# Seven block products instead of eight in the up projection of an fp32 transformer step

## The chip, the cores and the metric

The kernel runs on one core of a Trainium2 chip, in one launch. The metric is device time in microseconds (us). The core has a TensorE (PE in the profile: matmuls, and PEld, the load of their weights), a VectorE (DVE), a ScalarE (ACT), a GpSimd (POOL) and a SyncE (SP) that issues nearly all DMAs. Each takes its instructions in the order in which they stand; they meet at semaphores.

## The reference

One layer of a decoder with d = 1024, for 2048 prompt tokens and 8 x 8 sample tokens that share all weights: windowed attention and a pooling mixer side by side, attention to 256 memory tokens, then the MLP that the change is about, and a final RMSNorm.

```python
h = _rmsnorm(x, g_ffn)
x = x + jnp.square(jax.nn.relu(h @ w_up)) @ w_down      # w_up 1024 x 4096, w_down 4096 x 1024
y = _rmsnorm(x, g_final)
```

All of it is fp32.

## The kernel before

**Tokens.** Three superblocks `s` = 0, 1, 2 of two token blocks each: 384 + 384, 256 + 256 (with the 64 sample tokens beside the second block in attention), 384 + 384. In each superblock follow the input projection ("in"), attention mixed with it, the output projection ("wo"), cross attention (matrices A and B), the up projection ("up", function `up`) and the down projection ("dn", function `down`). Activations lie transposed: 128 channels on the partitions, tokens along the free dimension. `x` (tiles `x0`, `x1`) holds the residual of the two blocks.

**Three matmuls for one.** Every fp32 operand is split into a rounded part and a rest (`hi`, `lo`, type fp32r). `mm3` and `dense` issue hi x hi, hi x lo and lo x hi into one PSUM tile, so a product of a 128-row weight chunk with a block of tokens costs three matmuls; lo x lo is left out.

**The MLP.** The hidden layer of 4096 is cut into 32 chunks of 128, in eight groups `g` of four. `up(g)` makes four chunks, each over k = 8 input chunks (24 matmuls for each token block); `up_evac` takes the PSUM tile: DVE relu and the factor `r3` of the norm, ACT square and rounding (`hi`), DVE the rest (`lo`). `down(g)` adds the product of the four hidden chunks with the weights to `x`, 8 output chunks of 12 matmuls each, one DVE addition from PSUM for each. The gain of the norm is multiplied into the input (`gain`), the norm itself (`r3`) only after the matmul. In superblock 1 both blocks go as one of 512 tokens; in superblock 2 the sample tokens join (through the DRAM buffer `x_s`), and the two blocks are 512 and 320 wide.

**Weights.** `Stream` loads them in a written order: a DMA of 512 KB into a slot `f`, on ACT the rounding into a slot `w`, on DVE the rest into another (`emit`; L134 and L135 of the profile). There are 12 slots `w`, 6 slots `f`, and at most 5 weights stand ready ahead of use.

**Order.** The code is written in a rough order, with work put off to later points (`later`, `flush`); a scheduler then sets the order of the instructions on each engine, within what the slots and the data allow. The first norm of the next superblock (`norm1`) is started while `down(6)` and `down(7)` still run.

Of the kernel before, what the change touches and what calls it, by code (L numbers as in the profile page):

```python
# [14 lines left out]
P = 128  # L15
# [36 lines left out]
def kernel(ctx: ExitStack, tc: tile.TileContext, io, nW=12, nF=6, nT=8):  # L52
# [11 lines left out]
    TS = Slots([sb(f"t{i}", 448) for i in range(nT)])  # L64
    XT = [sb("x0", 3136), sb("x1", 3584)]
# [5 lines left out]
    x_s = drp.tile([P, 8, 64], F32, name="x_s", tag="x_s")  # L71
# [44 lines left out]

    class Stream:
# [6 lines left out]
        def add(self, key, *raw, eng=None):  # L124
            self.items.append((key, raw, eng or nc.vector))

        def emit(self):
            key, raw, eng = self.items.popleft()
            th, tl = WS.get(), WS.get()
            r = FS.get()  # L130
            w = 1024 // len(raw)
            for i, src in enumerate(raw):
                nc.sync.dma_start(r[:, w * i:w * i + w], src)
            nc.scalar.copy(th[:], r[:, 0:1024])  # L134
            eng.tensor_tensor(tl[:], r[:, 0:1024], f32(th[:]), ALU.subtract)  # L135
# [29 lines left out]
    for s in range(3):  # L165
# [103 lines left out]
    class Act:  # L269

        def __init__(self, n, nk=8, more=()):
            self.n, self.nk = n, nk
            w, per = (NB, 4) if n <= NB else (512, 3)
            left = 2 * nk - 2 * len(more)
            self.h = [ACTS.get() for _ in range(-(-left // per))]
            self.t = [t[:, w * i:w * i + w] for t in self.h for i in range(per)][:left]
            self.t += [t[:, 512 * i:512 * i + 512] for t in more for i in range(2)]
# [4 lines left out]
        def lo(self, k, c0=0, c1=None):  # L282
            return self.t[self.nk + k][:, c0:self.n if c1 is None else c1]
# [20 lines left out]
    def dense(keys, blks, hi, lo, evac, head=2, tail=3, after=None, piece=8, seq=None, early=False):  # L304
# [3 lines left out]
        for c, b in seq or order(nch, head, tail, len(blks)):  # L308
# [193 lines left out]
    def norm1(bl, wait=2):  # L502
        n = bl.n
# [18 lines left out]
        later.append([wait, rest])  # L522

    def load_x(bl):
        nc.sync.dma_start(bl.xv[:, :, 0:bl.n], io["x"][:, bl.xo:bl.xo + 8 * bl.n].rearrange("p (k n) -> p k n", n=bl.n))
        if bl.nf > bl.n:
            nc.sync.dma_start(bl.xv[:, :, bl.n:bl.nf], x_s[:])

    def superblock(s, blks, nxt):
# [486 lines left out]
        def sample_cross():  # L1016
# [117 lines left out]
            nc.sync.dma_start(x_s[:], bl.xv[:, :, bl.np:bl.n])  # L1134
# [7 lines left out]
        def add_evac2(c, b, ps):  # L1142
            bl = blks[b]
            nc.vector.tensor_tensor(bl.x(c, 0, bl.np), ps[:, 0:bl.np], bl.x(c, 0, bl.np), ALU.add)
            for p in bl.parts:
                gain(p.x(c), p.fb.h3.hi(c, p.o, p.o + p.n), p.fb.h3.lo(c, p.o, p.o + p.n), vec[:, V_GFFN + c:V_GFFN + c + 1])
            bl.norm.sq(c)

        def after_co(b):
            bl = blks[b]  # L1150
            for hf in range(2):
                ACTS.put(*bl.pt[hf])
            bl.norm.fin()
# [20 lines left out]
        if last:
            assert len(VS.free) == 4
            fbs[0].more = [(vt, WS.get()), (WS.get(),), (WS.get(),)]
        for fb in fbs:
            fb.h3 = Act(fb.n, 8, fb.more[0])

# [5 lines left out]
        run(dense([("B", s, c) for c in range(8)], pbs,  # L1185
# [3 lines left out]
        hid = {}  # L1189

        def up_evac(g):
            def f(c, b, ps):
                fb = fbs[b]
                if (g, b) not in hid:
                    hid[(g, b)] = Act(fb.n, 4, fb.more[1 + g % 2])
                H = hid[(g, b)]
                for p in fb.parts:
                    o, n = p.o, p.n
                    r, q = TS.get(), TS.get()
                    nc.vector.scalar_tensor_tensor(r[:, 0:n], ps[:, o:o + n], 0.0, p.bl.r3[:, p.c0:p.c0 + n], ALU.max, ALU.mult)  # L1200
                    nc.scalar.activation(q[:, 0:n], r[:, 0:n], AF.Square)  # L1201
                    hi, lo = H.hi(c, o, o + n), H.lo(c, o, o + n)
                    nc.scalar.copy(hi, q[:, 0:n])  # L1203
                    nc.vector.tensor_tensor(lo, q[:, 0:n], f32(hi), ALU.subtract)  # L1204
                    TS.put(r, q)
            return f
# [212 lines left out]
```

## Time and profile before

| | |
|---|---|
| runs | 2574.15, 2576.71, 2580.68 us; median 2576.71 us |
| profiled execution | 2575.38 us, of which the span from the first to the last instruction is 2573.6 us |
| granted TensorE clock | 0.996 |
| busy, share of the span | PE 98%, PEld 90%, DVE 54%, ACT 39%, POOL 7% |
| instructions | PE 14241 matmuls, DVE 2797, ACT 2013 |
| DMA | 245.09 MB, 95 GB/s on average |

A busy time is the time in which at least one instruction of the engine was under way. Matmuls overlap, so the mean duration of one (some 340 ns for 384 tokens) is its latency; the time that one costs in a stream is the length of a stretch of like matmuls over their number. In the profile's groups the shape is (partitions x elements), and "idle before" is the idle time of that engine just before the group.

### The profile page before, as it was taken

To read this page: it belongs to the slowest core of one execution; us is meant where nothing else is said; L and a number is where in the kernel's file an instruction comes from. 1 tells how busy PE (TensorE), PEld (TensorE's weight loads), DVE (VectorE), ACT (ScalarE), POOL (GpSimd) and SP (SyncE) were. 2 spreads that over 40 slices of the span, in tenths; PEclk is the share of its full clock that TensorE was granted. 3 is DMA by queue.
4 is the path that set the end of the run, shared out by engine and by line. 5 is a ranking of instruction groups with operands and counts; after the bars stand their busy time and mean duration, and the time that the engine had idled before them with its cause. 6 is when DMAs were issued, how large, how long until landed. Compare 5 with 4: busy or idle time off the path is not lost.

```text
span 2573.6 us, 36150 instructions
## 1 busy us (share of the span) xinstructions
PE 2534.6 (98%) x14241; PEld 2315.0 (90%) x14241; DVE 1388.7 (54%) x2797; ACT 998.9 (39%) x2013; POOL 167.4 (7%) x282
## 2 busy tenths in 40 slices
PE   9999999999999999999999999999999999999997
PEld 8798989999999999896788888899989888888886
DVE  8568545444434468774554546887445444434435
ACT  6666343322222234753442324475344322222222
POOL 0015010000000000411000000024010000000000
PEclk9999999999999999999999999999999999999999
DMA  8833212111111125146722222414111111111101
GB/s 284 266 121 102 91 37 78 66 66 66 58 65 66 50 66 160 50 168 213 283 98 93 97 99 75 155 32 148 42 62 54 66 58 58 63 60 58 58 25 54
DMA packets 97614, 245.09 MB, mean 95 GB/s; under 512 B 18916, under 2 KB 37796, under 8 KB 96420
## 3 DMA queue, kind: packets, MB, share of 16 engines
q1 hardware_dynamic: 97444, 242.78, 28.3%
q8 instruction: 112, 1.84, 0.3%
q14 instruction: 58, 0.48, 0.1%
HBM read 219.79 MB, written 22.95 MB: 94 GB/s over the span
## 4 chain that ended last, share of the span: by engine, by line
PE 56%; DVE 2%; ACT 1%; DMA 1%; POOL 0%; issue 0%; DVEq 0%; POOLq 0%; ACTq 0%
PE mm L318 10%; PE mm L317 10%; PE mm L319 10%; PE mm L114 7%; PE mm L113 7%; PE mm L115 7%; PE aux L724 1%; PE aux L755 1%; DVE x L1253 0%; PE aux L968 0%; PE aux L1052 0%; PE aux L114 0%; DVE w L135 0%; PE aux L113 0%; PE aux L115 0%; PE aux L1090 0%
## 5 line engine op out<-in xcount | busy, mean ns | idle before, releaser
L317 PE MATMUL mm<-act,w 128*128 128x384 f32 (+3 forms) x2528 | 857.1, 339 | 2.5 <-ACT act L679 1.6
L319 PE MATMUL mm<-act,w 128*128 128x384 f32 (+3 forms) x2528 | 851.4, 337 | 1.9 <-DVE w L135 1.9
L318 PE MATMUL mm<-act,w 128*128 128x384 f32 (+3 forms) x2400 | 801.8, 334 | 0.7 <-DVE act L680 0.7
L134 ACT CAST w<-f 128x1024 fp32r<-128x1024 f32 x330 | 346.5, 1051 | 818.2 <-PE mm L114 278.3
L113 PE MATMUL mm<-act,w 128*128 128x384 f32 (+3 forms) x1472 | 506.1, 344 | 3.2 <-ACT t L204 2.2
L115 PE MATMUL mm<-act,w 128*128 128x384 f32 (+3 forms) x1472 | 504.8, 343 | 1.9 <-DVE w L135 1.9
L317 PEld LDWEIGHTS mm<-act,w 128*128 128x128 f32 x2528 | 476.7, 189 | 28.3 <-ACT act L679 1.9
L319 PEld LDWEIGHTS mm<-act,w 128*128 128x128 f32 x2528 | 476.4, 188 | 23.1 <-DVE w L135 2.7
L135 DVE TENSOR_TENSOR w<-f,w 128x1024 fp32r<-128x1024 f32 x330 | 402.7, 1225 | 154.7 <-ACT w L134 76.9
L318 PEld LDWEIGHTS mm<-act,w 128*128 128x128 f32 x2400 | 452.6, 189 | 21.1 <-issue 2.5
L114 PE MATMUL mm<-act,w 128*128 128x384 f32 (+3 forms) x1344 | 454.1, 338 | 0.0
L1235 DVE TENSOR_TENSOR x<-mm,x 128x384 f32<-128x384 f32 (+2 forms) x448 | 199.2, 468 | 297.3 <-PE mm L115 297.2
L113 PEld LDWEIGHTS mm<-act,w 128*128 128x128 f32 x1472 | 277.1, 188 | 25.3 <-ACT t L204 2.4
L115 PEld LDWEIGHTS mm<-act,w 128*128 128x128 f32 x1472 | 277.1, 188 | 23.0 <-DVE w L135 2.3
L114 PEld LDWEIGHTS mm<-act,w 128*128 128x128 f32 x1344 | 253.0, 188 | 15.8
L1200 DVE SCALAR_TENSOR_TENSOR t<-mm,t 128x384 f32<-128x384 f32 (+3 forms) x224 | 99.8, 468 | 275.6 <-PE mm L319 275.5
L1201 ACT ACTIVATE t<-t 128x384 f32<-128x384 f32 (+3 forms) x224 | 95.1, 450 | 249.8 <-DVE t L1200 249.8
L1204 DVE TENSOR_TENSOR act<-t,act 128x384 fp32r<-128x384 f32 (+3 forms) x192 | 87.8, 477 | 88.9 <-ACT act L1203 88.9
L113 PE MATMUL mm<-w,act 128*128 128x512 f32 x288 | 114.8, 402 | 1.4 <-ACT w L134 1.3
L114 PE MATMUL mm<-w,act 128*128 128x512 f32 x288 | 113.1, 393 | 1.9 <-DVE w L135 1.8
L115 PE MATMUL mm<-w,act 128*128 128x512 f32 x288 | 112.8, 392 | 0.0
L266 ACT ACTIVATE act<-x,vec 128x384 fp32r<-128x384 f32 (+3 forms) x104 | 57.7, 563 | 106.5 <-DVE x L940 56.4
(210 smaller groups left out, 2200.5 us busy)
## 6 DMA issues: line engine op xcount, KB each, us to landing
f<-in_wup SPq DMA_DIRECT2D x96, 512.0 KB, 3.3
f<-in_wdn SPq DMA_DIRECT2D x96, 512.0 KB, 3.2
f<-in_win SPq DMA_DIRECT2D x30, 512.0 KB, 3.5
f<-a_s SPq DMA_DIRECT2D x24, 512.0 KB, 4.2
f<-b_s SPq DMA_DIRECT2D x24, 512.0 KB, 4.2
x<-in_x SPq DMA_DIRECT2D x6, 1536.0 KB, 8.1
f<-in_wco SPq DMA_DIRECT2D x16, 512.0 KB, 5.3
f<-in_cmk SPq DMA_DIRECT2D x16, 512.0 KB, 4.2
```

The costliest lines, as they stand in the source:

```text
L113: nc.tensor.matmul(ps, Wh(k), Hh(k), start=first and i == 0, stop=False)
L114: nc.tensor.matmul(ps, Wh(k), Hl(k), start=False, stop=False)
L115: nc.tensor.matmul(ps, Wl(k), Hh(k), start=False, stop=final and i == last)
L134: nc.scalar.copy(th[:], r[:, 0:1024])
L135: eng.tensor_tensor(tl[:], r[:, 0:1024], f32(th[:]), ALU.subtract)
L317: nc.tensor.matmul(ps[:, 0:n], w8(th)[:, k, :], hi(b, k), start=k == 0, stop=False)
L318: nc.tensor.matmul(ps[:, 0:n], w8(th)[:, k, :], lo(b, k), start=False, stop=False)
L319: nc.tensor.matmul(ps[:, 0:n], w8(tl)[:, k, :], hi(b, k), start=False, stop=k == 7)
L1200: nc.vector.scalar_tensor_tensor(r[:, 0:n], ps[:, o:o + n], 0.0, p.bl.r3[:, p.c0:p.c0 + n], ALU.max, ALU.mult)
L1201: nc.scalar.activation(q[:, 0:n], r[:, 0:n], AF.Square)
L1204: nc.vector.tensor_tensor(lo, q[:, 0:n], f32(hi), ALU.subtract)
L1235: nc.vector.tensor_tensor(p.x(m), ps[:, p.o:p.o + p.n], p.x(m), ALU.add)
```

## The change

The 1024 x 4096 up weight is seen as 16 pairs `p` of hidden chunks. For a pair, the weight is a 2 x 2 matrix of blocks (two halves of the 1024 input channels, two hidden chunks), the input a 2 x 2 matrix of blocks (two halves of the channels, two equal halves of the superblock's tokens). Their product takes seven block products and block sums (Winograd's form of Strassen's algorithm) where it took eight.

- **Token halves** are 384 in superblocks 0 and 2 and 288 in superblock 1 (256 + 32 and 288), where the sample tokens now stay: `x_s` is gone, and superblock 2 has no extra tokens.
- **Sums of inputs**: `B11`, `B21`, `T1`, `T2`, `B22`, `T3`, `T4`, each as hi and lo, made on DVE and ACT once in a superblock, during and just after the product with B (`sums0`, `sums1`, `sums2`); B's chunks come in the order 0, 4, 1, 5, 2, 6, 3, 7 so that the two halves of the channels meet. They lie in 14 of the 16 slots `act`.
- **Sums of weights**: `add_up` loads the pair's two chunks `g.c`, `g.d` and makes three stream items: the split of `g.c`; a DVE sum, a DVE difference and the split of `g.e`; a half split, two more DVE sums and the split of `g.d`. That is three full splits and a half instead of two, and four DVE sums of 512 columns.
- **Sums of outputs**: `up(p)` makes the products into `aux` tiles (which `up` did not use before), each over k = 4 (12 matmuls), and combines them by seven DVE additions and one ACT copy; then relu, square, hi and lo as before (`relu2`).
- **Down projection**: in superblocks 0 and 2 for each pair by itself, k = 2 chunks (6 matmuls for a PSUM tile, one DVE addition for each tile); in superblock 1 for two pairs together (k = 4, 12 matmuls); the last two pairs of each superblock together, one token half after the other.
- **Next superblock's norm**: its first block is started between the last two `up`, its second (`hook`) in the middle of the last `down`. Before, both were started before `down(7)`.
- Slots `t` are 10 of 400 columns instead of 8 of 448.

```diff
+            def first():
+                g.c, g.d = FS.get(), FS.get()
+                nc.sync.dma_start(g.c[:, 0:1024], io["wup"][2 * p])
+                nc.sync.dma_start(g.d[:, 0:1024], io["wup"][2 * p + 1])
+                return split(g.c)
+            def second():
+                g.e = FS.get()
+                nc.vector.tensor_tensor(g.e[:, 0:512], g.d[:, 0:512], g.d[:, 512:1024], ALU.add)
+                nc.vector.tensor_tensor(g.e[:, 512:1024], g.c[:, 0:512], g.e[:, 0:512], ALU.subtract)
+                return split(g.e)
...
+        def sums1(i):
+            e, d = TS.get(), TS.get()
...
+            gain(d[:, 0:hn], T("T1", 0)(i), T("T1", 1)(i), gk(i))
...
-        def up(g):
-            run(dense([("up", s, g, c) for c in range(4)], fbs,
-                      lambda b, k: fbs[b].h3.hi(k), lambda b, k: fbs[b].h3.lo(k), up_evac(g),
+        def up(p, H=None):
...
+            wa = S.next(("up", s, p, 0))
+            p1 = prod(wa, (0, 0), "B11")
+            r1 = TS.get()
+            nc.scalar.copy(r1[:, 0:hn], p1[:, 0:hn])
...
+            wb = S.next(("up", s, p, 1))
+            p5 = prod(wb, (0, 0), "T1")
+            p6 = prod(wb, (512, 512), "T2")
+            r2 = add(TS.get(), p6, r1)
+            r4 = add(TS.get(), p5, r2, False)
+            w22, *wd = S.next(("up", s, p, 2))
+            add(r4, prod(wd, (512, 512), "B22"), r4)
+            relu2(H, 1, 0, r4)
+            p7 = prod(wd, (0, 0), "T3")
+            add(r2, p7, r2)
+            relu2(H, 1, 1, add(TS.get(), p5, r2))
+            p2 = prod(wa, (512, 512), "B21")
+            relu2(H, 0, 0, add(r1, p2, r1))
+            p4 = prod((w22, w22), (0, 512), "T4")
+            relu2(H, 0, 1, add(r2, p4, r2))
...
-                    mm3(ps[:, 0:n], range(4), lambda k: w8(th)[:, 4 * m2 + k, :], lambda k: w8(tl)[:, 4 * m2 + k, :], H.hi, H.lo)
+                    mm3(ps[:, 0:hn], K, lambda k: w8(w[k // 2][0])[:, 2 * m4 + k % 2, :], lambda k: w8(w[k // 2][1])[:, 2 * m4 + k % 2, :],
...
+            for p in range(NP - 2):
+                up(p, H)
+                down([p], [H])
+        up(NP - 2, H)
+        if nxt is not None:
+            S.resF = 4
+            rest0 = norm1_sums(nxt[0])
+        H2 = up(NP - 1)
...
+            later.append([1, rest0])
+            hook = lambda i: norm1(nxt[1], 1) if i == 5 else None
+        down([NP - 2, NP - 1], [H, H2], True, hook)
```

Three places show what the scheduler makes of it. In the rows, L119 is the DVE half of a weight split (L135 before), L190 and L192 are sums of weights, L1292 a sum of outputs from PSUM, L1276 the relu and L1280 the lo part of `relu2` (L1200 and L1204 before), L1350 the addition to `x` in `down` (L1235 before).

On DVE, where an `up` of superblock 0 passes into a `down`, before:

```order
L1200 SCALAR_TENSOR_TENSOR t_101<-mm_107,t_104 128x384
L135 TENSOR_TENSOR w_82<-f_95,w_83 128x1024
L1204 TENSOR_TENSOR act_70<-t_98,act_69 128x384
L1200 SCALAR_TENSOR_TENSOR t_99<-mm_108,t_97 128x384
L1204 TENSOR_TENSOR act_68<-t_100,act_67 128x384
L1200 SCALAR_TENSOR_TENSOR t_102<-mm_109,t_104 128x384
L135 TENSOR_TENSOR w_84<-f_96,w_85 128x1024
L1204 TENSOR_TENSOR act_70<-t_103,act_69 128x384
L1235 TENSOR_TENSOR x_105<-mm_110,x_105 128x384
L1235 TENSOR_TENSOR x_105<-mm_107,x_105 128x384
```

and now, at the last products of a pair (`aux_115` is B21, `aux_116` is T4):

```order
L1292 TENSOR_TENSOR t_98<-aux_115,t_98 128x384
L1276 SCALAR_TENSOR_TENSOR t_104<-t_104,t_106 128x384
L1276 SCALAR_TENSOR_TENSOR t_98<-t_98,t_105 128x384
L1292 TENSOR_TENSOR t_100<-aux_116,t_100 128x384
L192 TENSOR_TENSOR f_91<-f_96,f_92 128x512
L1276 SCALAR_TENSOR_TENSOR t_100<-t_100,t_105 128x384
L1280 TENSOR_TENSOR act_74<-t_104,act_74 128x384
L1280 TENSOR_TENSOR act_73<-t_98,act_73 128x384
L1350 TENSOR_TENSOR x_108<-mm_112,x_108 128x384
L1350 TENSOR_TENSOR x_108<-mm_109,x_108 128x384
L1280 TENSOR_TENSOR act_73<-t_100,act_73 128x384
L119 TENSOR_TENSOR w_86<-f_91,w_79 128x1024
```

Three lo parts that `down` needs now stand behind the sum that waits for T4, the last product, and one of them behind the first two additions of `down`.

On DVE, where superblock 1 ends and the input projection of superblock 2 begins, before:

```order
L540 TENSOR_TENSOR w_84<-kcar,w_85 64x128
L1235 TENSOR_TENSOR x_105<-mm_107,x_105 128x256
L1235 TENSOR_TENSOR x_106<-mm_107,x_106 128x256
L135 TENSOR_TENSOR w_86<-f_93,w_88 128x1024
L208 TENSOR_TENSOR t_98<-t_98,t_97 128x256
L208 TENSOR_TENSOR t_100<-t_100,t_101 128x256
L99 TENSOR_TENSOR w_90<-mm_109,w_89 64x384
```

and now (L263 to L265 are the end of a norm, L300 and L302 the normalised input of the next superblock's second block, L250 the sums of squares and L1371 the output of the final norm; 15 rows like the last five stand between the two pieces):

```order
L1350 TENSOR_TENSOR x_108<-mm_109,x_108 128x288
L263 SCALAR_TENSOR_TENSOR t_100<-t_97 128x384
L263 SCALAR_TENSOR_TENSOR t_103<-t_101 128x256
L264 SCALAR_TENSOR_TENSOR t_100<-aux_113,t_100 128x384
L264 SCALAR_TENSOR_TENSOR t_103<-aux_114,t_103 128x256
L265 SCALAR_TENSOR_TENSOR t_97<-t_100,t_97 128x384
L265 SCALAR_TENSOR_TENSOR t_101<-t_103,t_101 128x256
L300 SCALAR_TENSOR_TENSOR t_105<-f_96,vec,t_97 128x384
L300 SCALAR_TENSOR_TENSOR t_98<-f_96,vec,t_97 128x384
L1371 SCALAR_TENSOR_TENSOR x_107<-x_107,vec,t_101 128x256
L302 TENSOR_TENSOR act_69<-t_105,act_77 128x384
```

```order
L302 TENSOR_TENSOR act_70<-t_102,act_78 128x384
L1371 SCALAR_TENSOR_TENSOR x_107<-x_107,vec,t_101 128x256
L300 SCALAR_TENSOR_TENSOR t_105<-f_94,vec,t_97 128x384
L300 SCALAR_TENSOR_TENSOR t_98<-f_94,vec,t_97 128x384
L119 TENSOR_TENSOR w_85<-f_93,w_87 128x1024
L302 TENSOR_TENSOR act_70<-t_105,act_78 128x384
```

Before, the normalised input was made long before this place; now it is made here, behind the last addition of `down`, and the second weight of the input projection (`w_85`) stands behind it.

On PE, in the input projection of superblock 2 after the change, 44 matmuls after the last one of `down`:

```order
L353 MATMUL mm_109<-act_70,w_80 128x384
L354 MATMUL mm_109<-act_78,w_88 128x384
L352 MATMUL mm_109<-act_78,w_80 128x384
L354 MATMUL mm_112<-act_64,w_85 128x384
L352 MATMUL mm_112<-act_64,w_87 128x384
L353 MATMUL mm_112<-act_67,w_87 128x384
```

PE turns to the second block (`mm_109`, input `act_69`, `act_70`) after the first 24 matmuls, and the fourth of these rows, its 48th matmul after `down`, reads `w_85`; before, all four first weights and both inputs were there, and it went from chunk to chunk.

More of the change, by code (lines that the diff above doesn't have):

```diff
@@ L115, in mm3, with split @@
             nc.tensor.matmul(ps, Wl(k), Hh(k), start=False, stop=final and i == last)
+    def split(r):
+        th, tl = WS.get(), WS.get()
+        nc.scalar.copy(th[:], r[:, 0:1024])
+        nc.vector.tensor_tensor(tl[:], r[:, 0:1024], f32(th[:]), ALU.subtract)
+        return th, tl
+    class FB:
+        pass
     class Stream:
@@ L269, with __init__ @@
     class Act:
[L271 to L277, printed above, removed]
+        def __init__(self, n):
+            self.n = n
+            self.h = [ACTS.get() for _ in range(4)]
+            self.t = [t[:, NB * i:NB * i + NB] for t in self.h for i in range(4)]
         def hi(self, k, c0=0, c1=None):
@@ new lines, in superblock, with tslots, T, f @@
+        hn = halves[1][0][3]
+        PT = 288 if has else NB
+        NAMES = ("B11", "B21", "T1", "T2", "B22", "T3", "T4")
+        tt = {}
+        def tslots(i2, names):
+            for nm in names:
+                tt[(nm, i2)] = ACTS.get()
+        def T(nm, hl):
+            def f(i, c0=0, c1=hn):
+                o = PT * (2 * (i % 2) + hl)
+                return tt[(nm, i // 2)][:, o + c0:o + c1]
+            return f
+        def xp(h, k):
+            return [(bl.x(k, c0, c0 + w), slice(o, o + w), o, o + w) for bl, c0, o, w in halves[h]]
@@ L1174, in superblock @@
[L1174 to L1178, printed above, removed]
+            blks[b].norm.fin()
+            blks[b].r3 = blks[b].norm.r
+        for bl in blks:
+            bl.norm = Norm(bl.n, bl.x)
+        tslots(0, NAMES)
         pbs = []
@@ L1184, in superblock @@
             pbs.append(q)
-        run(dense([("B", s, c) for c in range(8)], pbs,
+        run(dense([("B", s, c) for c in BO], pbs,
                   lambda b, k: k4(blks[b].pt[k // 4][0], blks[b].np)[:, k % 4, :],
                   lambda b, k: k4(blks[b].pt[k // 4][1], blks[b].np)[:, k % 4, :], add_evac2, tail=2, after=after_co))
[L1189 to L1206, printed above, removed]
@@ L1249, in final, with own, relu2 @@
-        def final(p):
-            p.norm.fin()
-            n, yo = p.n, 8 * (p.bl.t0 + p.c0)
+        def own(ts):
+            return [t[:, PT * i:PT * i + hn] for t in ts for i in range(4)]
+        def relu2(H, h, k, t):
+            for bl, c0, o, w in halves[h]:
+                nc.vector.scalar_tensor_tensor(t[:, o:o + w], t[:, o:o + w], 0.0, bl.r3[:, c0:c0 + w], ALU.max, ALU.mult)
+            nc.scalar.activation(t[:, 0:hn], t[:, 0:hn], AF.Square)
+            hi, lo = H[4 * h + 2 * k], H[4 * h + 2 * k + 1]
+            nc.scalar.copy(hi, t[:, 0:hn])
+            nc.vector.tensor_tensor(lo, t[:, 0:hn], f32(hi), ALU.subtract)
+            TS.put(t)
```

317 lines of the change are left out of this document (188 added, 129 removed).

## The prediction

> **What bounds the kernel now.** The page comes first: span, engines, granted clock, and the shares of the chain that ended last.
>
> ```profile
> span 2573.6 us, 36150 instructions
> PE 2534.6 (98%) x14241; PEld 2315.0 (90%) x14241; DVE 1388.7 (54%) x2797; ACT 998.9 (39%) x2013; POOL 167.4 (7%) x282
> PEclk9999999999999999999999999999999999999999
> PE 56%; DVE 2%; ACT 1%; DMA 1%; POOL 0%; issue 0%; DVEq 0%; POOLq 0%; ACTq 0%
> ```
>
> PE is under way nearly always, and nothing else has weight in the chain. A busy PE need not be at its peak, so the second view is stretches of like matmuls: 384 wide, 512, 320, 256 (first four rows), a pause of PE and what follows it (two rows), then the three MLPs and the two passages from one superblock to the next. Columns: length, then busy time and number by engine, clock, DMA.
>
> ```profile
> 500.00:890.00 390.00, 390.00 (x2252) 390.00 (x2251) 158.81 (x235) 94.98 (x139) 0.00 (x0) 1.00 0.19 62
> 1350.00:1550.00 200.00, 200.00 (x884) 165.60 (x883) 98.28 (x183) 61.03 (x109) 0.00 (x0) 1.00 0.29 97
> 998.50:1018.50 20.00, 20.00 (x138) 20.00 (x138) 16.63 (x36) 8.09 (x15) 1.47 (x3) 1.00 0.71 234
> 1263.00:1296.00 33.00, 33.00 (x276) 32.95 (x275) 24.63 (x47) 17.98 (x35) 0.00 (x0) 1.00 0.54 187
> 1031.00:1035.00 4.00, 2.60 (x19) 1.67 (x17) 2.45 (x6) 2.49 (x8) 2.66 (x4) 0.99 0.00 0
> 1035.00:1037.00 2.00, 2.00 (x11) 2.00 (x10) 1.05 (x3) 1.17 (x4) 0.00 (x0) 0.50 0.33 94
> 455.00:993.00 538.00, 538.00 (x3112) 537.26 (x3111) 249.59 (x404) 154.48 (x254) 3.50 (x5) 1.00 0.20 68
> 1298.00:1648.00 350.00, 350.00 (x1545) 289.42 (x1544) 201.50 (x392) 129.13 (x250) 0.00 (x0) 1.00 0.31 102
> 1980.00:2541.00 561.00, 561.00 (x2977) 498.93 (x2976) 231.06 (x454) 141.84 (x271) 0.00 (x0) 1.00 0.16 52
> 990.00:1019.00 29.00, 29.00 (x209) 28.73 (x208) 24.25 (x50) 11.94 (x23) 3.74 (x7) 1.00 0.73 213
> 1648.00:1680.00 32.00, 32.00 (x186) 31.90 (x185) 22.92 (x45) 11.69 (x23) 0.79 (x3) 1.00 0.37 120
> ```
>
> Length over number (less the one or two cut at the ends): 384 wide 173.3 ns, 512 wide 226.7, 320 wide 146, 256 wide 120. The steps fit 13.3 ns + 0.4167 ns for each token, which gives 133.3 ns for 288. PE never pauses in an MLP or in the passages; what a matmul fewer saves there is its whole time, while the others follow.
>
> **PE's work in the change.** Up, 32 chunks x 8 k x 3 = 768 matmuls for each token block before; 16 pairs x 7 products x 12 = 1344 for each superblock now. Down, 768 for each block before, 8 tiles x 2 halves x 96 = 1536 now.
>
> - Superblock 0, up: 1536 x 173.3 = 266.2 before, 1344 x 173.3 = 232.9 now: -33.3 us. Down: 1536 x 173.3 both times.
> - Superblock 1 (512 before, twice 288 now). Up: 768 x 226.7 = 174.1, 1344 x 133.3 = 179.2: +5.1. Down: 174.1, 1536 x 133.3 = 204.8: +30.7.
> - Superblock 2 (512 and 320 before, twice 384 now). Up: 768 x (226.7 + 146.7) = 286.8, 232.9: -53.9. Down: 286.8, 266.2: -20.6.
>
> The sum is -72.0 us. 288 has no row; bounds are 120 and 146 (256 and 320 wide), so 2880 matmuls leave +-38 us between them, but four widths on one line leave the middle, +-2.
>
> The Trainium skill's "TensorE: Matmul & The Clock Gate" (Back-to-back issue gap) gives N / 2.4 + 2.5 ns for a warm matmul and so a fixed part of 2.5 ns, not 13.3. By it the many narrow matmuls would cost less and the sum would be an estimated -82 us; the rows (173.3 where it gives 162.5) decide against it.
>
> **DVE's work beside it.** Prices come from the groups (latency, an upper price) and the timeline (start to start, what one costs in a queue).
>
> ```profile
> L135 DVE TENSOR_TENSOR w<-f,w 128x1024 fp32r<-128x1024 f32 x330 | 402.7, 1225 | 154.7 <-ACT w L134 76.9 <-PE mm L318 37.9 <-PE mm L114 32.6
> L1235 DVE TENSOR_TENSOR x<-mm,x 128x384 f32<-128x384 f32 x192 | 106.6, 556 | 204.7 <-PE mm L115 204.7
> L99 DVE TENSOR_TENSOR act<-aux,act 128x512 fp32r<-128x512 f32 x50 | 34.3, 685 | 7.2 <-ACT act L98 4.6
> L267 DVE SCALAR_TENSOR_TENSOR act<-x,vec,act 128x384 fp32r<-128x384 f32 x52 | 32.0, 616 | 16.4 <-ACT act L266 16.4
> L1235 DVE TENSOR_TENSOR x<-mm,x 128x256 f32<-128x256 f32 x128 | 48.9, 419 | 55.9 <-PE mm L115 55.7
> L1201 ACT ACTIVATE t<-t 128x384 f32<-128x384 f32 x96 | 50.3, 524 | 218.8 <-DVE t L1200 218.8
> L134 ACT CAST w<-f 128x1024 fp32r<-128x1024 f32 x330 | 346.5, 1051 | 818.2 <-PE mm L114 278.3 <-PE mm L318 213.8 <-PE mm L115 205.9
> 638.81 1.23 DVE L135 TENSOR_TENSOR w<-f,w 128x1024 fp32r<-128x1024 f32 x1 [0.35 <-ACT w L134]
> 639.95 0.55 DVE L1204 TENSOR_TENSOR act<-t,act 128x384 fp32r<-128x384 f32 x1
> 656.59 0.55 DVE L1204 TENSOR_TENSOR act<-t,act 128x384 fp32r<-128x384 f32 x1
> 657.06 0.55 DVE L1235 TENSOR_TENSOR x<-mm,x 128x384 f32<-128x384 f32 x1
> 2554.84 4.32 DVE L1253 SCALAR_TENSOR_TENSOR x<-x,vec,t 128x384 f32<-128x384 f32 x8
> ```
>
> In a queue a split costs 1.14 us (638.81 to 639.95), a 384-wide operation 0.47 (656.59 to 657.06), one with a scalar vector 0.53 (4.32 over 8), 512 columns about 0.6 (between).
>
> A pair in superblocks 0 and 2 lasts 84 + 96 = 180 matmuls, 31.2 us of PE. DVE does 5 splits (3 up, 2 down), 4 sums of weights, 7 sums of outputs, 8 operations of `relu2` and 16 additions to `x` (8 before): 5 x 1.14 + 4 x 0.6 + 31 x 0.47 = 22.7 us, 73%; at the latencies 26.5, and with 0.35 us of waiting for ACT at each split 28.2, 90%. ACT: 3.5 + 2 splits and 9 operations, 5.5 x 1.05 + 9 x 0.52 = 10.5 us. Two pairs of superblock 1 last 2 x 84 + 192 = 360 matmuls, 48 us; DVE does 10 splits, 8 sums of weights, 30 operations 288 wide (about 0.37) and 24 narrower ones (about 0.25): 33.3 us, 69%. So DVE has room everywhere, and the DMAs are as many as before, at a share of 0.2.
>
> Room is not order. Where a pair of superblock 0 ends, DVE waits for T4 and then needs 0.47 + 0.6 + 0.47 (sum of T4, weights, relu) and 0.47 for T3's lo, 2.0 us. PE has in that time the first input chunk of four output tiles, 12 matmuls, 2.1 us, and two of the next pair and four that need only hi, 1.0 us more. T4's lo comes after B21's lo and two additions, some 4.9 us, and is needed after 5.2. So nothing waits, with 0.3 to 1 us to spare. In superblock 1, from T2 of the first pair to T4 of the second PE has 11 products of 1.6 us, 17.6; DVE has 7 splits, 3 sums of weights and 30 operations there, 21 us. It ends some 4 us behind, and PE first needs that work 6.4 us later, at the second token half. I charge 0.1 us for each of 32 pairs, 0.5 for each of 8 double pairs and 1 us for the three starts of the MLP: +8 us, between 0 and 0.6 us for each of 48 pairs (+29), the spare of the first walk.
>
> The 36 DVE operations on the inputs, for 16 before, lie beside B, 384 matmuls, 66.6 us, where DVE has some 90 operations and 8 splits, 52 us. The last need 5.7 us after B; T2, T3 and T4 need them later than that. Nothing is charged.
>
> **The passages.** Here cover goes: the norm of the next second block is made in the last `down` and after it, not before `down(7)`. After superblock 1 the weight `w_85` stands behind 1 addition (0.37), 6 norm operations (2.8), 8 normalisations (4.2), 6 lo parts (2.8), 6 of the final norm at 256 (0.41 each, 2.5), 4 sums of squares (1.6) and its own split (1.14): 15.4 us after `down`. PE has 47 matmuls before it, 8.2 us. It waits 7.2 us, in pieces. After superblock 0 the fourth PSUM tile from the end is added, then 28 operations of that kind stand before the next addition, 12 us from 6.1 us before the end of `down` on; PE's first chunk (24 x 0.12) is done at 2.9, the second needs that tile: 3 us.
>
> The clock pays too: after 4 us in which PE was busy for 2.60 it was granted 0.50 (1031 to 1037 above). The first passage looks like that, so I add 2 us there. Both: +12 us, between 0 (if the final norms, which nobody needs, are quick or the lag is made up later) and 20 (7.2 + 3, and 3.4 us of half clock at three places).
>
> **The end.** The last matmul, and what DVE did before and after it:
>
> ```profile
> 2558.05 0.31 PE L115 MATMUL mm<-act,w 128*128 128x320 f32 x1
> 2562.90 2.19 DVE L1253 SCALAR_TENSOR_TENSOR x<-x,vec,t 128x128 f32<-128x128 f32 x8
> 2566.58 3.79 DVE L1253 SCALAR_TENSOR_TENSOR x<-x,vec,t 128x320 f32<-128x320 f32 x8
> ```
>
> It took 15.2 us from the end of the last matmul (2558.4) to 2573.6, with two final norms one after the other. Now one is left: an addition behind the other norm (1.5), square, matmul, two ACT operations (2.5), three DVE (1.7), eight (4.3), the output (3.2): 13.2. -2 us.
>
> **The sum**, against the profiled execution's own 2575.4 us (1.3 under the median of 2576.7, 1.8 outside the span): -72.0 - 2 + 8 + 12 = -54.0, so 2521.4, **2521 us**.
>
> **Rivals.**
> - *All is hidden.* DVE's 73% and 69% speak for it, the passages' order against it. 2575.4 - 74 = 2501.
> - *DVE is late at each pair.* The spare is 0.3 us and the 21 us against 17.6 in superblock 1 are real; against it stands that PE never waited in an MLP so far. At the upper bound, 29 us for 8: 2542; with as much again at the weights: 2560.
> - *The clock falls in the MLP, and it gets slower.* If a lo part or an addition comes late by 1.4 us in each pair, PE is busy for 2.6 of 4 us once in 31, and by the pair of rows at 1031 it is then granted 0.50 for some 3.4 us: 1.7 us more. 48 x 3.1 = 149 us instead of 8: 2662. It decides from (74 - 12) / 48 = 1.3 us for each pair on. The clock's 1.00 in all MLP rows speaks neither way, since PE never paused there. The same page of the Trainium skill (Part 1, the clock gate) says that the clock is halved after an idle window of about 3.4 us; the rows above agree on the half, though PE there was partly busy.
>
> The matmuls themselves are not in doubt: 4032 and 4608 of them stand in the order.
>
> **Chances.** The forecast (2508 to 2540) 0.57; all hidden (below 2508) 0.13; late pairs (2540 to 2569) 0.17; within 0.3% (2569 to 2584, about what this measurement tells from no change) 0.04; slower, by the clock, 0.09. So faster 0.87, same 0.04, slower 0.09. The range of eight in ten leaves out the slow case and half of the late pairs' upper part: 2500 to 2552.
>
> **What would show it.** Windows of the MLPs: 499 us (superblock 0), 384 (1) and 499 (2) and some 8 more between them, with PE busy throughout and 173 and 133 ns for a matmul. DVE at 70 to 75% there. In the waits, PE for DVE (L1280, L1350) near nothing; at the passages PE behind L119 and L1350 for some 10 us. I am wrong if a matmul 288 wide costs far from 133 ns, if PE waits for L1280, L1292 or L1350 in every pair, or if the clock falls below 1.00 in an MLP.

## The result and the profile after

The changed kernel takes 2538.17 us (median of 4, 2537.34 to 2544.59) against 2578.69 us of the kernel before (median of 4): ratio 0.985, 95% interval 0.9826 to 0.9873. Forecast were 2521 us, in a range of 2500 to 2552. The profiled execution took 2537.34 us, 38.0 less than the one before; the forecast of its sum was 54.0 less. So the gain is there, and 16 us of it are missing. The page says little about them:

```profile
span 2535.3 us, 38897 instructions
PE 2483.3 (98%) x15199; PEld 2368.2 (93%) x15199; DVE 1858.8 (73%) x3687; ACT 1098.6 (43%) x2131; POOL 172.5 (7%) x282
PE 78%; DVE 4%; ACT 1%; DMA 1%; POOL 1%; issue 0%; POOLq 0%; DVEq 0%; ACTq 0%
```

PE is busy for 98% as before, with DVE up from 54% to 73%. The sight that helps is the execution cut into stages. PE's order gives the borders: first matmul of the first `up`, last matmul of the last `down`. Stretches of the kernel before, then after: MLP of superblock 0, everything up to the next MLP, MLP of superblock 1, everything up to the next, MLP of superblock 2 (length, then busy time and number by engine, clock, DMA).

```profile
454.00:988.80 534.80, 534.80 (x3083) 534.06 (x3082) 246.14 (x399) 153.03 (x251) 0.42 (x1) 1.00 0.20 66
988.80:1296.90 308.10, 301.51 (x2116) 260.85 (x2115) 194.65 (x461) 153.38 (x344) 52.44 (x92) 0.98 0.51 173
1296.90:1647.00 350.10, 350.10 (x1544) 289.35 (x1543) 201.59 (x393) 129.12 (x249) 0.00 (x0) 1.00 0.31 103
1647.00:1977.40 330.40, 328.11 (x1849) 308.31 (x1848) 207.66 (x467) 163.89 (x372) 56.00 (x87) 1.00 0.22 74
1977.40:2558.40 581.00, 580.96 (x3088) 515.99 (x3086) 241.55 (x474) 147.18 (x280) 0.00 (x0) 1.00 0.15 51
```

```profile
453.20:959.90 506.70, 506.70 (x2890) 499.74 (x2890) 401.24 (x699) 175.52 (x293) 0.00 (x0) 1.00 0.22 69
959.90:1274.40 314.50, 303.90 (x2117) 262.04 (x2116) 210.99 (x512) 162.51 (x369) 53.23 (x93) 0.98 0.50 170
1274.40:1668.50 394.10, 389.56 (x2891) 386.70 (x2890) 316.89 (x684) 166.50 (x293) 0.00 (x0) 1.00 0.26 88
1668.50:2011.80 343.30, 335.38 (x1848) 311.56 (x1847) 235.90 (x516) 174.95 (x391) 57.23 (x87) 0.99 0.24 79
2011.80:2521.20 509.40, 509.40 (x2896) 500.40 (x2894) 386.84 (x658) 161.54 (x257) 0.00 (x0) 1.00 0.18 60
```

| stage | forecast, us | measured, us |
|---|---|---|
| MLP of superblock 0 | -31.4 (-33.3 matmuls, +1.9 late) | -28.1 |
| to the MLP of superblock 1 | +3 | +6.4 |
| MLP of superblock 1 | +40.1 (+35.8, +4.3) | +44.0 |
| to the MLP of superblock 2 | +9.2 (7.2 waits, 2 clock) | +12.9 |
| MLP of superblock 2 | -72.6 (-74.5, +1.9) | -71.6 |
| end | -2 | -1.1 |

(Before the first MLP: -0.8.) The signs and the order of sizes are those of the forecast; nearly every stage gives back 1 to 4 us more. Two kinds of place are behind it. In nearly every pair of superblocks 0 and 2 PE starts the first matmuls of `down` late. Weight loads of PE in one pair, then ACT in the 3 us before:

```profile
565.39 0.65 PEld L112 LDWEIGHTS mm<-act,w 128*128 128x128 f32 x4 [0.27 <-ACT act L1279]
568.28 0.19 PEld L113 LDWEIGHTS mm<-act,w 128*128 128x128 f32 x1 [0.16 <-DVE act L1280]
```

```profile
563.05 1.05 ACT L118 CAST w<-f 128x1024 fp32r<-128x1024 f32 x1 [3.26 <-PE aux L114]
564.00 0.93 ACT L1277 ACTIVATE t<-t 128x384 f32<-128x384 f32 x2
564.84 0.91 ACT L1279 CAST act<-t 128x384 fp32r<-128x384 f32 x2
```

The hi part of T3 (L1279) is 0.27 us late, because ACT, idle for 3.26 us, began a weight split (L118, 1.05 us) just as the relu of T3 came; the lo part (L1280) is 0.16 us late behind two additions. Matmul by matmul, the spacing above the even one adds up to some 0.34 us, at 13 pair ends in each of these two superblocks (26 in all).

The other kind are three borders: just after the MLP of superblock 0, just after that of superblock 1, and at the start of the MLP of superblock 1. Their stretches, and what PE mainly waited for in each (the first row of waits for the first, two for the second, one for the third):

```profile
960.00:972.00 12.00, 9.13 (x54) 8.96 (x53) 12.00 (x26) 6.36 (x12) 3.62 (x5) 0.72 0.86 240
1668.00:1690.00 22.00, 17.65 (x73) 13.95 (x72) 21.88 (x45) 9.80 (x19) 0.64 (x2) 0.84 0.57 182
1276.00:1296.00 20.00, 15.80 (x101) 14.73 (x100) 18.24 (x42) 12.11 (x24) 0.00 (x0) 0.91 0.24 79
PE mm L352 <- DVE x L1350: 2.9, 1, 2.9
PE mm L352 <- ACT act L301: 2.4, 4, 1.2
PE mm L353 <- DVE act L302: 1.2, 3, 0.4
PE aux L112 <- DVE t L264: 2.7, 1, 2.7
```

DVE is busy almost without a pause there (12.00 of 12, 21.88 of 22, 18.24 of 20). PE was idle for 2.9, 4.4 and 4.2 us, 11.4 in all, and the granted clock fell to 0.72, 0.84 and 0.91: 0.28 x 12 + 0.16 x 22 + 0.09 x 20 = 8.7 us of clock, an upper figure, since part of that time was idle. In a second execution of the kernel the first of the three is 0.86, so it varies.

### The profile page after: what moved, and what is told of

The parts are those of the page before. It is cut to its first block, busy times and chain, and to the rows that moved or that the text cites. A ratio compares the mean times of both kernels' runs of the same rounds, so it can differ in the third digit from the quotient of the medians.

```text
span 2535.3 us, 38897 instructions
## 1 busy us (share of the span) xinstructions
PE 2483.3 (98%) x15199; PEld 2368.2 (93%) x15199; DVE 1858.8 (73%) x3687; ACT 1098.6 (43%) x2131; POOL 172.5 (7%) x282
## 4 chain that ended last, share of the span: by engine, by line
PE 78%; DVE 4%; ACT 1%; DMA 1%; POOL 1%; issue 0%; POOLq 0%; DVEq 0%; ACTq 0%
PE mm L112 11%; PE mm L113 11%; PE mm L114 11%; PE aux L112 9%; PE aux L113 9%; PE aux L114 9%; PE mm L352 5%; PE mm L354 5%; PE mm L353 5%; PE aux L754 1%; PE aux L785 1%; DVE x L1371 1%; PE aux L1082 0%; ACT w L118 0%; DVE t L300 0%
## 5 line engine op out<-in xcount | busy, mean ns | idle before, releaser
L118 ACT CAST w<-f 128x1024 fp32r<-128x1024 f32 x378 | 395.6, 1050 | 731.5 <-PE mm L114 366.6
L119 DVE TENSOR_TENSOR w<-f,w 128x1024 fp32r<-128x1024 f32 x378 | 460.4, 1222 | 185.6 <-PE aux L113 98.3
L113 PE MATMUL mm<-act,w 128*128 128x384 f32 (+2 forms) x1728 | 552.8, 320 | 0.0
L114 PE MATMUL mm<-act,w 128*128 128x384 f32 (+2 forms) x1728 | 550.7, 319 | 0.8 <-DVE w L119 0.8
L112 PE MATMUL mm<-act,w 128*128 128x384 f32 (+2 forms) x1728 | 537.9, 321 | 3.4 <-DVE t L459 2.2
L112 PE MATMUL aux<-act,w 128*128 128x384 f32 (+1 forms) x1344 | 432.4, 322 | 3.6 <-DVE t L264 2.7
L114 PE MATMUL aux<-act,w 128*128 128x384 f32 (+1 forms) x1344 | 432.1, 322 | 0.0
L113 PE MATMUL aux<-act,w 128*128 128x384 f32 (+1 forms) x1344 | 431.9, 321 | 0.0
L352 PE MATMUL mm<-act,w 128*128 128x384 f32 (+2 forms) x1248 | 408.7, 328 | 7.3 <-DVE x L1350 2.9
L354 PE MATMUL mm<-act,w 128*128 128x384 f32 (+2 forms) x1248 | 405.1, 325 | 3.2 <-DVE w L119 3.1
L353 PE MATMUL mm<-act,w 128*128 128x384 f32 (+2 forms) x1248 | 405.9, 325 | 1.6 <-DVE act L302 1.2
L1350 DVE TENSOR_TENSOR x<-mm,x 128x384 f32<-128x384 f32 (+3 forms) x672 | 313.8, 493 | 125.8 <-PE mm L114 124.1
L112 PEld LDWEIGHTS mm<-act,w 128*128 128x128 f32 x1728 | 322.8, 189 | 13.3 <-ACT act L1279 7.0
L113 PEld LDWEIGHTS mm<-act,w 128*128 128x128 f32 x1728 | 326.5, 189 | 5.4 <-DVE act L1280 3.8
L114 PEld LDWEIGHTS mm<-act,w 128*128 128x128 f32 x1728 | 326.1, 189 | 2.0 <-DVE w L119 1.0
L112 PEld LDWEIGHTS aux<-act,w 128*128 128x128 f32 x1344 | 252.7, 188 | 4.8 <-DVE t L264 3.2
L114 PEld LDWEIGHTS aux<-act,w 128*128 128x128 f32 x1344 | 253.4, 189 | 0.3
L113 PEld LDWEIGHTS aux<-act,w 128*128 128x128 f32 x1344 | 253.5, 189 | 0.0
L352 PEld LDWEIGHTS mm<-act,w 128*128 128x128 f32 x1248 | 238.8, 191 | 13.7 <-issue 3.9
L353 PEld LDWEIGHTS mm<-act,w 128*128 128x128 f32 x1248 | 238.7, 191 | 7.4 <-DVE act L302 2.8
L354 PEld LDWEIGHTS mm<-act,w 128*128 128x128 f32 x1248 | 238.5, 191 | 5.6 <-DVE w L119 4.9
L1292 DVE TENSOR_TENSOR t<-aux,t 128x384 f32<-128x384 f32 (+1 forms) x336 | 169.4, 517 | 24.4 <-PE aux L114 18.7
```

The costliest lines, as they stand in the source:

```text
L112: nc.tensor.matmul(ps, Wh(k), Hh(k), start=first and i == 0, stop=False)
L113: nc.tensor.matmul(ps, Wh(k), Hl(k), start=False, stop=False)
L114: nc.tensor.matmul(ps, Wl(k), Hh(k), start=False, stop=final and i == last)
L119: nc.vector.tensor_tensor(tl[:], r[:, 0:1024], f32(th[:]), ALU.subtract)
L352: nc.tensor.matmul(ps[:, 0:n], w8(th)[:, k, :], hi(b, k), start=k == 0, stop=False)
L353: nc.tensor.matmul(ps[:, 0:n], w8(th)[:, k, :], lo(b, k), start=False, stop=False)
```

## Experiments

Times are medians of 4 runs each, beside the kernel before on the same chip; it took 2574.65 to 2576.05 us in the four groups. Stages are compared between single profiled executions. The base is the changed kernel in one of the groups:

> The changed kernel again, beside the others: its ratio to the kernel before and its stages are the base for the small differences. 2538 us within 5, stages within 2 us of the first profile; all theories say the same.

2539.34 us, ratio 0.9853 (0.9838 to 0.9868); its stages in the order above 506.6, 314.9, 394.2, 341.7, 509.4, within 2 us of the first profile. MLP stages repeat within 0.1 us, the ones between within 1.6, so differences below 2 us are read in MLP stages only.

**Eight products with all else changed.** The stream has two plain splits for a pair, the input only `B11`, `B21` and the two blocks of the other half, and `up` four PSUM tiles of 24 matmuls:

```diff
-            add_up(s, p)
+            S.add(("up", s, p, 0), io["wup"][2 * p])
+            S.add(("up", s, p, 1), io["wup"][2 * p + 1])
...
+            wc = S.next(("up", s, p, 0))
+            p1 = prod(wc, 1)
...
+            relu2(H, 0, 1, prod(wd, 0))
...
```

> Eight products in the up projection, no sums of weights, inputs or outputs; the token halves of 384, 288, 384, the down projection and the norms stay. PE has 192 matmuls more for each superblock and token width: 16 x 12 x (173.3 + 133.3 + 173.3 ns) = 92.1 us. Theory A (the time that PE loses in the MLPs, some 28 us, comes from the sums): about 20 of them go, 2538 + 92 - 20 = 2610 us. Rival B (the loss belongs to the down projection by pairs and to the norms): 2538 + 92 = 2630 us. Against the kernel before, the forecast of the parts gives +20 (halves) + 14 (passages, end): 2611.

2607.28 us, 1.013 (1.0115 to 1.0145) of before, 67.9 more than the changed kernel, near theory A's 2610. The three MLPs:

```profile
450.10:985.30 535.20, 535.18 (x3081) 533.84 (x3080) 295.22 (x491) 149.77 (x242) 0.00 (x0) 1.00 0.19 62
1300.60:1712.60 412.00, 412.00 (x3083) 410.91 (x3082) 211.39 (x463) 135.89 (x237) 0.00 (x0) 1.00 0.24 80
2052.80:2590.60 537.80, 537.80 (x3088) 534.73 (x3086) 280.27 (x450) 135.52 (x206) 0.00 (x0) 1.00 0.16 54
```

The matmuls alone would take 532.4, 409.6 and 532.4 (3072 of 173.3 or 133.3 ns), so 2.8, 2.5 and 5.4 us are lost, against 7.5, 10.2 and 10.3 with seven products: seven products with their sums lose 17 us more in the MLPs. The stages between stay at 315.3 and 340.2. What is lost there belongs to the moved norms and the new halves, not to the sums. The halves, the down projection and the moved norms by themselves make the kernel 32 us slower; the seven products win back 68, net of what their sums lose.

**Weight sums made three times.** The first two sums in a loop of three, 2.4 us of DVE more in each pair:

```diff
-            nc.vector.tensor_tensor(g.e[:, 0:512], g.d[:, 0:512], g.d[:, 512:1024], ALU.add)
+            for _ in range(3):
+                nc.vector.tensor_tensor(g.e[:, 0:512], g.d[:, 0:512], g.d[:, 512:1024], ALU.add)
...
+            for _ in range(3):
+                nc.vector.tensor_tensor(g.e[:, 512:1024], g.c[:, 0:512], g.e[:, 0:512], ALU.subtract)
```

> The first two of the four sums of weights are each made three times, so DVE has 4 x 0.6 = 2.4 us more in each pair: 25.1 of 31.2 us in superblocks 0 and 2. Theory A (only the order at a pair's end makes PE wait, DVE has room): within 0.2 us for each of 48 pairs and 2 us at the starts, at most +10 us. Rival (DVE is near its limit, so what it does more goes into the time): half of 48 x 2.4 us or more, +60 us.

2544.51 us, 5.2 more than the base, within theory A's 10. MLPs of superblocks 0 and 1:

```profile
454.10:960.70 506.60, 506.60 (x2889) 499.65 (x2889) 431.64 (x756) 175.59 (x293) 0.00 (x0) 1.00 0.20 69
1275.90:1677.30 401.40, 392.35 (x2893) 389.47 (x2892) 352.67 (x752) 169.51 (x296) 0.00 (x0) 0.99 0.25 86
```

In superblock 0 DVE is busy for 30 us more and the time stays at 506.6 to the tenth. In superblock 1 it rises by 7.2 us, by the spacing of the matmuls all within the first 40 us. So more work on DVE costs nothing in the run of pairs, and it does cost time where DVE starts behind.

**Fewer additions at the borders.** Left out: of the squares of each norm ahead of, in and after the MLP only the first and the last are added.

```diff
-                self.add.tensor_tensor(self.acc[:, 0:n], self.acc[:, 0:n], t[:, 0:n], ALU.add)
+                if not self.skip or k == 7:
+                    self.add.tensor_tensor(self.acc[:, 0:n], self.acc[:, 0:n], t[:, 0:n], ALU.add)
...
+            bl.norm.skip = True
...
```

> Left out: of the eight squares of each norm at the borders of the MLP only the first and the last are added up, so DVE does 6 additions less in each of 15 norms, 4.4 us in the B of superblock 1, 5 to 5.6 at the other borders for each pair of norms, and the chain from the last square to the norm's end stays as it is. Theory C (DVE is full and behind at the borders, and PE pays what DVE does there one for one): the MLP of superblock 1 391 us instead of 394, the stage after superblock 0 311 instead of 315, the one after superblock 1 335 instead of 342; about 2539 - 15 = 2524 us. Rival D (it is the length of the chains of norms, additions and splits behind each other, not the amount of DVE's work): 1 us less at most at each place, 2537 us.

2524.73 us, ratio 0.9802 (0.9786 to 0.9819), 14.6 below the base. The MLP of superblock 1 takes 387.9 (-6.3), the stages between 313.6 (-1.3) and 337.7 (-4.0). The start of that MLP, and the first 22 us after it:

```profile
1276.00:1296.00 20.00, 18.82 (x140) 18.39 (x139) 19.90 (x44) 13.10 (x24) 0.00 (x0) 1.00 0.29 98
1663.50:1685.50 22.00, 21.67 (x121) 20.47 (x120) 21.43 (x44) 12.75 (x24) 0.67 (x3) 1.00 0.52 180
```

The idle time falls from 4.2 to 1.2 and from 4.4 to 0.3 us, and the clock stays at 1.00. At the start of the MLP, 4.4 us of DVE are worth 6.3, since the half clock goes with the wait. After superblock 0 the gain is a third of what was expected: PE still waits there 2.1 us for the addition to `x` (2.9 in the base), at a clock of 0.86 in both.

**Two ways to move the wait at that start.** First the last input sums after the second product:

```diff
+            bl.norm.sq(c)
             if pos == 7:
...
-                    sums2(2)
-                    sums2(3)
+                    later.append([3, lambda: [sums2(2), sums2(3)] and None])
...
-            bl.norm.sq(c)
```

> The last T3 and T4 of the inputs are made after the second product of the first pair, and the square for the norm comes ahead of the input sums. Theory A (at the start of the MLP in superblock 1 PE waits because DVE still makes input sums, so the norm that holds a PSUM tile is late): 2538 - 5 = 2533 us, the 6.7 us lost at that start fall below 2. Rival B (the norm's own chain of about 4 us, from its matmul to its release of the tile, is what holds the third product): the start loses 5 us or more still, 2538 us within 2.

2539.88 us, MLP of superblock 1 394.2: no gain, so theory A's time fails. Then the PSUM tile that PE waits for (L264 releases it) from the other pool:

```diff
...
             bl.norm = Norm(bl.n, bl.x)
+            bl.norm.ps = MM
```

> The mean square of the second norm of a superblock's cross attention goes to one of the four PSUM tiles of the dense products (free at that place), not to one of the four tiles of the block products. Theory B, from the run with late sums (at the start of the MLP the third product waits for the tile that the norm holds for 3 to 4 us): the start of the MLP in superblock 1 loses 2 us, not 6.7, the others 0.3 less, about -5 us. Rival A (the input sums are late): -1 us at most.

2537.54 us, MLP of superblock 1 394.1: theory B fails too. What PE waited for at the start, with late sums (three rows) and with the other tile (one), and the first 20 us with late sums, cut as above:

```profile
PE aux L112 <- ACT act L1200: 0.9, 1, 0.9
PE aux L113 <- DVE act L1201: 0.7, 1, 0.7
PE aux L112 <- DVE t L264: 0.6, 1, 0.6
PE aux L112 <- DVE t L1294: 4.4, 2, 2.4
1278.80:1298.80 20.00, 17.73 (x102) 16.10 (x101) 18.41 (x42) 12.37 (x24) 0.00 (x0) 0.83 0.23 79
```

With the cause named taken away, the next thing that is made is late: input sums (L1200, L1201), or sums of outputs (L1294 is L1292 of the changed kernel). The releaser in the list names who comes last, not why. With late sums the wait for L264 did fall from 2.7 to 0.6 us, as theory A has it, and PE's idle time from 4.2 to 2.3; but there are more short waits, the granted clock is 0.83 over these 20 us against 0.91, and the MLP is as long as before. Of the three, only less work (above) made this MLP shorter.

**ACT's order at a pair's end.** The two slots of the first split come free after that of the half split, so the next weight split can't start before T4 is done:

```diff
-            WS.put(*wa)
             relu2(H, 0, 0, add(r1, p2, r1))
...
             WS.put(w22)
+            WS.put(*wa)
```

> The slots of the first split come free after that of the half split, so that the weight split that now stands ahead of T3's relu on ACT falls behind it. Theory A (the 0.34 us lost in each pair of superblocks 0 and 2 come from that split on ACT, 1.05 us, ahead of the hi part of T3): some 8 of the 9.5 us in 28 pairs go, 2530 us. Rival B (DVE, busy for 24 of 31 us, is late at the pair's end by itself): the 0.3 us stay and the releaser becomes DVE's lo part, 2538 us within 2.

2534.92 us, ratio 0.9849 (0.9832 to 0.9865): by the runs not told from the base. By the stages, the MLPs of superblocks 0 and 2 take 503.9 and 506.6, -2.7 and -2.8; that of superblock 1 takes 394.9, +0.7. ACT and PE's weight load in one pair:

```profile
561.26 1.00 ACT L1277 ACTIVATE t<-t 128x384 f32<-128x384 f32 x2 [0.95 <-DVE t L1276]
562.16 0.91 ACT L1279 CAST act<-t 128x384 fp32r<-128x384 f32 x2
562.98 1.04 ACT L118 CAST w<-f 128x1024 fp32r<-128x1024 f32 x1
562.71 0.65 PEld L112 LDWEIGHTS mm<-act,w 128*128 128x128 f32 x4 [0.17 <-ACT act L1279]
```

The split stands behind T3's hi part now, and DVE's lo part makes nobody wait. 0.14 of the 0.34 us stay: the load still waits for T3's hi part (last row), which comes at the end of a chain of two sums, relu, square and hi. Two thirds of theory A. Its median is the lowest of the versions that leave nothing out.

**An earlier norm for the next second block.**

```diff
-    PIECE = ((2, 2), (4, 4), (4, 4))
+    PIECE = ((8, 2), (4, 4), (4, 4))
...
-            hook = lambda i: norm1(nxt[1], 1) if i == 5 else None
+            hook = lambda i: norm1(nxt[1], 1) if i == 2 else None
```

> The norm of the next second block is made from step 2 of the last down on, not step 5, and that of the first block in one piece. Theory A (the passages lose time because this norm's DVE work stands ahead of the additions and of the weight w_85): the passage after superblock 0 loses 6.5 us less, the one after superblock 1 some 5 of its 10 us (the final norms stay), so 2538 - 11 = 2527 us. Rival B (the norm only moves its cost into the last down, or the weights are late anyway): the last down of each superblock gets longer by as much, 2538 us within 3.

2548.91 us: the stages between fall to 310.4 and 332.2 (-4.5 and -9.5), as theory A says, but the MLPs ahead of them rise to 516.6 and 410.6 (+10.0 and +16.4). With pieces of (4, 2) and step 3:

> The norm of the next second block from step 3 of the last down on, after the second pair of down weights has its slots; the first block's norm in two pieces. From the run with step 2 (passages 4 and 11 us shorter, but the last down 10 and 16 us longer, PE behind the split L118): if that price was the weights of down standing behind the norm for a slot f, it goes, and the passages stay short: -10 to -15 us against the changed kernel. Rival (the slots f are too few for any earlier place): the last down stays 5 us or more longer, and the gain is 0 to 5.

2541.16 us: stages between 316.1 and 336.4, MLPs 507.5 and 400.7. PE in the last `down` of each (step 2, superblocks 0 and 1), and around the end of superblock 1 with step 3:

```profile
PE mm L112 <- ACT w L118: 8.0, 1, 8.0
PE mm L112 <- ACT w L118: 10.8, 1, 10.8
PE mm L112 <- DVE x L1350: 4.8, 1, 4.8
PE mm L352 <- DVE x L1350: 3.4, 1, 3.4
```

At step 2 the second pair of weights stood behind the norm, and PE paid 8 and 10.8 us for the split. At step 3 that is gone, and DVE's additions are late in the last `down` in place of the norm after it: -5.3 us behind superblock 1, +6.5 in it. Neither of the two earlier places is free on DVE.

**Additions on POOL**, which is mostly idle there (busy for 3.62, 0.64 and 0.00 us in the three stretches above):

```diff
-            bl.norm = Norm(bl.n, bl.x)
+            bl.norm = Norm(bl.n, bl.x, add=nc.gpsimd)
```

(and the same for the norms in and after the last `down`)

> The additions of squares for the norms ahead of the MLP, after it and in the last down (14 x 0.33 to 0.47 us in each place) are made on POOL, which is idle there, not on DVE. Theory C (at the borders of the MLP DVE is busy without a pause and some 7 us behind, and whatever it does less there PE gains): the start of the MLP in superblock 1 loses 2 to 3 us instead of 7, the passage after superblock 0 2 instead of 6.5, the one after superblock 1 4 to 5 instead of 10; 2539 - 14 = 2525 us. Rival (the additions on POOL take 0.6 to 0.9 us by its rows, so the chains to the norms get longer, or DVE gets slower beside it): 2539 us within 4, with waits for L250 on PE.

> Additions of squares on POOL, the norm's tile among those of the dense products, and the half split's slot ahead of the first split's. Theory C: the gains add up, -14 -1 -5.5 us against the changed kernel, 2518 us. Rival (each removes the same wait): 2525 us.

> As the three together, and the norm of the next second block from step 3 of the last down. Theory C (the place of that norm mattered nothing while DVE was full; now there is room in the last down, so an earlier place shortens the passages and costs less): 3 to 6 us below the three together, 2514 us. Rival (DVE is still full in the last down): the same within 2.

2557.53, 2550.40 and 2554.17 us: 11 to 18 us slower than the base. The first goes the way of its rival, and by more; the other two miss both of their times. Additions on POOL by size, what PE waited for in the whole execution, and a single addition beside DVE:

```profile
L250 POOL TENSOR_TENSOR t<-t,t 128x384 f32<-128x384 f32 x63 | 70.6, 1121 | 960.8 <-ACT t L249 947.4 <-DVE w L119 13.0
L250 POOL TENSOR_TENSOR t<-t,t 128x320 f32<-128x320 f32 x21 | 24.5, 1169 | 43.0 <-ACT t L249 40.8 <-issue 1.8
PE aux L258 <- POOL t L250: 20.0, 7, 6.0
1290.26 3.02 POOL L250 TENSOR_TENSOR t<-t,t 128x320 f32<-128x320 f32 x1 [3.32 <-ACT t L249]
1292.47 1.11 DVE L1224 SCALAR_TENSOR_TENSOR t<-x,vec,t 128x288 f32<-128x288 f32 x1
```

An addition takes 1.1 us there against 0.55 on DVE, and the one shown, beside DVE's unbroken queue, 3.02; the norm's matmul stands in PE's order and waits for the additions, 20 us at seven places. DVE had less to do and PE won nothing, because the additions are in the chain to PE. The three together are 7 us better than the additions on POOL alone (the new ACT order again gives 3 in each outer MLP); with the earlier norm the kernel is 3.8 us slower still, which the runs don't tell apart.

## Why the prediction was right, and where it fell short

- *The matmuls, -72.0.* Right. In the middle of the MLP of superblock 1 (first row below) 2400 matmuls stand in 320 us, 133.3 ns each, as worked out for a width without a row. With eight products that whole MLP takes 134.1 ns for a matmul.
- *Room is not order: 0.1 us for each pair.* That the order at a pair's end costs time, and not the amount of DVE's work, was right. The path was wrong and the price a third: some 0.34 us at 26 pair ends, about 9 us where 3.2 were charged. The working followed DVE's queue and took ACT as free (10.5 us of 31); the 0.2 us that ACT's split adds were not in it, and the new ACT order shows them.
- *0.5 us for each double pair.* Too dear. The MLP of superblock 1 is 10.2 us longer than its matmuls; 6.9 of them lie at its start, and 2.5 are lost with eight products too, which leaves 0.8 for eight double pairs where 4 were charged. The first row below has no loss at all.
- *The 36 operations on the inputs, "nothing is charged".* Wrong, and the step that failed is plain: it set 52 us of DVE against the B of superblock 0, 66.6 us. In the last 66.6 us ahead of that MLP (second row) DVE is busy for 46.9, and the MLP starts without a pause of PE. In superblock 1 B is narrower, some 51 us; its last 50.4 (third row) have 47.0 of DVE, and the MLP starts with DVE behind: 6.9 us lost where I had a share of 1. Thrice the sums (+7.2 there, nothing in superblock 0) and fewer additions (-6.3) show that it is the amount of work; with eight products, without these sums, PE does not pause in that MLP.

```profile
1314.00:1634.00 320.00, 320.00 (x2400) 319.60 (x2399) 246.97 (x520) 123.62 (x205) 0.00 (x0) 1.00 0.27 90
386.60:453.20 66.60, 64.72 (x373) 63.90 (x372) 46.94 (x83) 30.35 (x55) 1.81 (x2) 1.00 0.15 48
1224.00:1274.40 50.40, 50.40 (x373) 44.87 (x372) 47.01 (x101) 36.12 (x68) 0.00 (x0) 1.00 0.54 195
```

- *Luck.* In the sum for the MLP of superblock 1 the 4 us charged too dearly for the double pairs hide part of the start that was left out; that this part came within 4 us is luck.
- *The passages, +12.* Measured +6.4 and +12.9. The waits at their starts were those forecast in kind: 2.9 us for the addition at L1350 (3 forecast), 4.4 us (7.2 forecast) after superblock 1, though there for the normalised input (L301, L302) and only 0.4 for `w_85`. Mis-sized was the clock: 2 us in one passage against up to 8.7 at three places, of which one is the start of an MLP. After each of these waits came some 3 to 6 us of matmuls spaced as at half clock.
- *Its own signs of being wrong.* Two of them came in small: in the pair shown above PE's load waits 0.16 us for L1280, and the clock falls below 1.00 at the start of the MLP of superblock 1. DVE is busy for 79, 80 and 76% of the three MLPs, where 70 to 75 were expected.
- *The end.* 14.1 us against 13.2, from 15.2.
- *The rivals.* All hidden (2501) and the clock in every pair (2662) did not come: the late 0.34 us are a quarter of the 1.3 us from which that would decide, and the clock is 1.00 over each outer MLP. Where PE did pause in an MLP, at 1280, the clock fell in the way that this rival has it:

```profile
1280.00:1284.00 4.00, 1.87 (x11) 1.12 (x9) 4.00 (x9) 1.46 (x4) 0.00 (x0) 1.00 0.00 0
1284.00:1288.00 4.00, 2.80 (x13) 2.80 (x14) 4.00 (x9) 1.25 (x2) 0.00 (x0) 0.72 0.00 0
```

The Trainium skill has in "TensorE: Matmul & The Clock Gate" (Part 1) that the clock is halved after an idle window of about 3.4 us. The trace agrees that the clock falls after a pause, but a shorter one did it here: PE was busy for 1.87 of these 4 us, and its longest wait was 2.7 us.

Of the +12.9 us after superblock 1 the waits and the clock at its start explain about 8. About 3 more stand where the cross attention of superblock 2 goes over into its B:

```profile
PE aux L998 <- POOL cp L1023: 1.9, 2, 1.3
1945.25 1.81 POOL L1023 TENSOR_SCALAR cp<-cp,st 128x256 f32<-128x256 f32 x2 [7.56 <-DVE st L1021]
1944.00:1952.00 8.00, 6.13 (x27) 5.58 (x26) 3.79 (x7) 2.00 (x5) 1.81 (x2) 0.79 0.17 61
```

PE waits there 1.9 us for two operations of POOL, which took 1.81 us together where they took 0.93 before the change (PE waited 0.3 us for them then), and the clock falls to 0.79 over 8 us. In the second execution the wait is 1.8 us and the clock stays at 1.00; that stage is 1.6 us shorter. DVE makes sums of weights for the next MLP at that time (L183, L184, L191), but no run tests whether they are the cause. Open stay the last 1 to 2 us of that stage, and why the addition after superblock 0 is still late with fewer additions.

## What to carry to other kernels

An engine at 73% can still be full at the borders of stages, and there its work goes into the time: taking an estimated 4.4 to 5.6 us (from the prices of the additions left out) off DVE at each of three borders was worth 6.3, 4.0 and 1.3 us, clock included. Cost a new load stage by stage, against the shortest stretch that has to cover it. Where an engine is behind, a wait that is moved came back at the next consumer, or in pieces with more half clock; take work away, and see that what takes it over isn't in the same chain. Fewer products for more sums paid here since the sums lie beside matmuls in the long stages: 68 us won, after 17 us lost with the sums.

## Not expected of the hardware

POOL's addition of 128 x 320 took 3.02 us beside a full DVE, and an operation of DVE (L1224) that takes 0.51 us in the changed kernel took 1.11 in the same moment. The Trainium skill ("GPSIMD Engine Reference", Specifications) says that POOL shares its interfaces to the memory (SBUF) with DVE, with contention where a DVE instruction has two inputs there, as this one has; the rows are in line with it, but no run here takes the two apart.
